# Another written-out order for an attention section of 958 steps, with three kinds of step free to change engine

## The chip, the cores and the metric

The kernel runs on one core of one Trainium2 chip. The time is the device time of one execution in microseconds (us). The engines are TensorE (PE; PEld is its weight load), VectorE (DVE), ScalarE (ACT), GpSimd (POOL) and SyncE (SP, which here only issues DMA transfers). L432 is line 432 of the kernel.

## The reference, cut to what matters

Two layers on an activation of 256 tokens by 1024 features, all in float32. Layer 0 is a gated linear recurrence and a squared-ReLU MLP. Layer 1 is sparse attention and a second MLP. A final norm follows.

```python
for i in range(DEPTH):                       # DEPTH = 2
    h = _rmsnorm(x, norm_mix[i])
    x = x + (_rglru_mixer(h, ...) if i % 2 == 0 else _nsa_mixer(h, ...))
    h = _rmsnorm(x, norm_ffn[i])
    x = x + _sq_relu_mlp(h, ...)             # relu(h @ w_up)**2 @ w_down
return _rmsnorm(x, norm_final)

# _nsa_mixer, 16 heads of 64 in 4 key/value groups
q, kv, gates = split(h @ w_in)
k_c, v_c = compress(kv[0]), compress(kv[1])  # blocks of 32 tokens, stride 16: gelu(flat @ w1) @ w2
p_c = softmax(q @ k_c - alibi);  p_s = softmax(q @ k_selected - alibi);  p_w = softmax(q @ k_window - alibi)
o = g0 * p_c @ v_c + g1 * p_s @ v_s + g2 * p_w @ v_w
return o @ w_out
```

With 256 tokens the window (512) and the selection (16 blocks of 64) leave no token out, so both branches differ only in keys, values and gates.

## The kernel before

**Products.** Activations lie with features on the 128 partitions and the 256 tokens along the free dimension. A float32 product is made of two parts of each operand: `hi`, the value rounded to the type that the matmul takes, and `lo`, the residue. `mm3` (L432 to L434) runs three matmuls per product (hi hi, hi lo, lo hi). A piece of weights (128x1024) is read from HBM into one of five `raw` buffers by a DMA on SyncE's queue (`load`, L365), its `hi` is a cast (L445, by ScalarE or VectorE), its `lo` a subtraction on VectorE (L442).

**The section.** The whole of layer 1's attention, from the projections to the first products of the following MLP, is one `Section`. `add(engines, cost, function, r, w, t)` registers a step, with the keys that it reads and writes, from which the dependencies follow; a step may list two engines. `emit(ORDER)` then issues the 958 steps one by one as the string `ORDER` (L59 to L92) names them; a `'` behind the number takes the step's second engine. The costs and the times `t` play no part in it. Each engine runs its own steps in that order, and so does each DMA queue: a step that must wait holds up all behind it on its engine.

```python
for x in seed.split():
    who, fn = self.tasks[int(x.rstrip("'"))][:2]
    fn(self.engines[who[x[-1] == "'"][0]])
```

**The steps of attention.** The projections (q, k, v and the two inputs of the compressed branch) are `mm3` products of weight pieces. Keys (`kh`, `kl`) and queries (`sa`, `sb`, with hi and lo) are scaled, cast and subtracted into place or first into `th` and `tl`, and then brought to the other partition half by DMA moves of 64 KB, issued by SyncE (L480). For each pair of head and branch group a step of scores (L1316, L1317) fills a bank of PSUM, VectorE adds the position bias and finds the row's extreme (L1323), ScalarE takes the exponential and the row sum (L1326), the probabilities `pt` are scaled (L1345, on either engine), transposed by TensorE (L1356) into a bank, copied to `pth` (L1359, ScalarE), their residue subtracted to `ptl` (L1360, VectorE), and multiplied by the values (L1381, L1383). The compressed branch adds its product into the same bank (L1253 for its scores, L1294 and L1388 for its values).

A pair of heads leaves its two half results in one bank: the lower head's result needs the upper partitions of one column block and the lower ones of the other. So for each half a copy (L1392, ScalarE) brings one block across the partitions into the tile `osum`, and an add (L1395, VectorE) adds the other block. `osum` is then split into `oh` (L445) and `ol` (L442) and goes into the output product, whose result is added to the residual `xt` (L659).

**The norm after it.** For each of the eight feature blocks: `hh`, the block scaled by the norm's weights (L570, ScalarE), its residue (L571, VectorE), a square (L574, ScalarE; the last block on VectorE) and its sum into `acc` (L581, VectorE). The MLP's first up projections run on the unscaled activation while `stats` (L643) sums `acc` over the partitions, and the scaling factor is spread by a product (L648).

Steps that the text names: 648, 738, 653 and 696 are score products; 637 the compressed branch's scores of a later pair; 851, 878 and 880 are L1392 copies of the last two pairs, 878 and 880 the two of the last; 935 a square of the norm; 27, 28, 36, 38, 39, 48, 253 casts of 64x256 into keys or queries; 514 and 621 casts of 128x256 into `th`; 139, 402, 859, 860 rescales of 128x128 and 140, 141 of 128x256; 244, 927, 967, 983, 1009 weight casts; 282 and 283 copies of the compressed hidden values; 758, 885, 965, 973 loads of weights; 581, 624, 627, 629 moves of two query blocks.

Of the kernel before, what the change touches and what calls it, by code (L numbers as in the profile page):

```python
# [14 lines left out]
AF = mybir.ActivationFunctionType  # L15
OP = mybir.AluOpType
# [39 lines left out]
551' 553 547 526 540 557 543 552 563 544 558 548 565 555 567 556 569 559 560 561 562  # L56
"""
ORDER = """
1 4 11 19 7 10 20 2 21 3 22 30 88 12 75 13 31 14 82 15 181 89 32 16 33 17 23 90 98 91 24' 83 92 41 27 18 42 34 194 29 43  # L59
38' 223 99 28 44 25 50 45 242 26 51 46 36' 164 35' 69 47 37 52 165 53 64 54 321 59 67 93 55 62 95 48 60 70 56 183 65 72  # L60
71 39 184 74 57 77 66 118 61 79 119 376 123 121 120 49 73 126 76 40 196 81 124 78 58 68 80 197 153 225 148 84 151 426 86
156 127 149 85 226 110 87 157 207 94 114 108 97 122 480 109 244' 101 128 152 96 129 100 150 111 132 102 6 323 130 133
208 134 103 210 135 9 131 105 0 166 125 154 63 107 115 155 104 136 142 106 137 211 140' 167 139' 378 245 168 141 169 143
116 175 505 324 138 185 428 161 170 158 566 112 146' 186 145' 162 144' 113 187 159 429 174 188 173 198 189 172 176 163
199 193 379 200 482 201 160 612 190 227 117 678 178' 192 202 217 228 483 507 229 171 191' 230 205 204' 246 231 203 247
147' 234' 235 248 508 206 249 218 232 212 233' 325 568 250 213 220 255 215 251 219 209 569 253 256 614 257 252 221 615
216 258 179 177 222 268 259 326 261 269 214 260 273 262 180 263 254 327 270 236 264 276 328 265 271 277 266 237 380 267
329 680 285' 278 330' 283' 370 333 274 279 373 282 281 284 381 280 335 331 272 681 240 286 336 275 338 241 299 310 290
238 758 287 291 382 311 300 288 292 313 430 301 312 289 315 296 383 314 302 293 297 349 716 303 354 384 294 304 239 340
350 385 305 357 341 306 390 355 371 352 392 431 307 374 394 885 356 308 410 375 432 351 397 309 411 358 316 484 413 395  # L70
317 353 298 423 386 414 399 318 295 433 388 319 400 372 424 469 925 402' 718 320 485 434 425 342 401 719 359 435 472 343
440 444 412 420 360 509 445 403 361 345 344 438 486 421 362 346 404 436 415 363 422 760 487 447 364 418 455 365 347 488
366 419 416 456 367 489 348 474 417 368 492 494 457 477 475 369 470 570 490 458 405 449 478 406 495 571 450 476 460 442
451 479 407 452 534 497 461 408 572 535 459 471 409 573 454' 462 537 536 473 904 464 510 574 538 784 463 453 524 467 575
511 465 527 468 525 512 466 539 528 580 540 526 499 513 887 761 588 585 529 586 616 500 514 532 501 530 541 515 503 519
531 587 542 520 617 589 888 522 543 631 533 618 517 544 632 965 619 590 545 502 633 581 596 504 620 591 927 583 560 634
546 576 592 549 561 621 594 599 564 622 597 563 550 593 626 648 658 562 551 629 651 595 552 685 649 635 578 553 565' 547
# [6 lines left out]
840 823 800 792 839 831' 807 793 822 824 789 794 796' 803 825 801 842 797' 832 795 828' 808 804 843 829' 830 845 844 790  # L84
731 802 846 835 863 841 833 848 847 805 732 834 866 791 836 849 806 864 857 850 858 865 867 917 862 861' 859' 909 860
868 853 809 869 851 872 854 870 889 852 873 871 896 947 874 875 967' 975 948 876 855' 856 877 983' 910 880 890 878 881
918 879 929 882' 930 883 897 968 919 891 931 892 911 1007 932 898 893 912 937 895 899 991 984 938 939 900 958 933 901
# [3 lines left out]
"""  # L91
ROUNDS, SHIFT, MOVES, SPREAD = 6, 1.5, 12, 3.0  # L92
HPEN, LPEN, APEN, LEAD = 0.56, 1.0, 0.0, 9.0
# [50 lines left out]
class Plan:  # L144
# [9 lines left out]
    def add(self, eng, dur, fn=None, r=(), w=(), t=0.0, lag=None):  # L154

        if fn is None:
            eng, fn = eng, dur
        if isinstance(eng, str):
            eng = [(eng, dur, 0.0)]
        i, deps = len(self.tasks), set()  # L160
        for k in r:
            if k in self.writer:
                deps.add(self.writer[k])
            self.readers.setdefault(k, []).append(i)
        for k in w:
            deps.update(self.readers.pop(k, ()))
            if k in self.writer:
                deps.add(self.writer[k])
            self.writer[k] = i
        deps.discard(i)  # L170
        self.tasks.append((eng, fn, sorted(deps), t, lag))
# [158 lines left out]
def trunk_kernel(ctx: ExitStack, tc: tile.TileContext, x_in, vec_in, const_in, w2_in, wts, out):  # L330
    nc = tc.nc
    ctx.enter_context(tc.manual_schedule())
    pe, dve, act, pool = nc.tensor, nc.vector, nc.scalar, nc.gpsimd
# [110 lines left out]
    def copy(o, a):  # L444
        return lambda e: (e.copy if e is act else e.tensor_copy)(o, a)  # L445
# [7 lines left out]
    class Section:  # L453
# [112 lines left out]
        def norm(self, m, gcol, t):  # L566

            g = vec[:, gcol + m:gcol + m + 1]
            xk = [("xt", m)]
            self.add("act", 0.4, lambda e: e.activation(hh[:, m], xt[:, m], AF.Identity, scale=g), r=xk, w=[("hh", m)], t=t)  # L570
            self.add("dve", 0.4, lambda e: e.scalar_tensor_tensor(  # L571
                hl[:, m], xt[:, m], g, hh[:, m].bitcast(F32), op0=OP.mult, op1=OP.subtract), r=xk, w=[("hh", m)], t=t)
            dst, dk = (acc, "acc") if m == 0 else (sqs[m % 2], ("sq", m % 2))
            sq = lambda e: (e.activation(dst, xt[:, m], AF.Square) if e is act else  # L574
                            e.tensor_tensor(dst, xt[:, m], xt[:, m], op=OP.mult))
            if m == KC - 1:
                self.add("dve", 0.34, sq, r=xk, w=[dk], t=t)
                return
            self.add("act", 0.31, sq, r=xk, w=[dk], t=t + 0.3)
            if m:  # L580
                self.add("dve", 0.34, lambda e: e.tensor_tensor(acc, acc, dst, op=OP.add), r=[dk], w=["acc"], t=t + 0.6)  # L581

# [401 lines left out]
    with ExitStack() as ph:  # L984
# [363 lines left out]
        def transposes(s, t):  # L1348
            pt = pts[s % NPT]
            for b in range(2):  # L1350
                bk = [("ps", 5 + b)]
                tp = zview(("tp", s, b), 5 + b, lambda x: x[:, :3 * P])

                def run(e, tp=tp, b=b):
                    for i, o in enumerate((b * P, 2 * P + b * S, 2 * P + b * S + P)):
                        e.transpose(tp()[:, i * P:(i + 1) * P], pt[:, o:o + P], identf)  # L1356
                add("pe", 0.25, run, r=[("pt", s % NPT, qc, b) for qc in range(2)], w=bk, t=t)
                i = s // 2 * 4 % NTH + 2 * b + s % 2
                add("act", 0.37, lambda e, tp=tp, i=i: e.copy(pth[i], tp()), r=bk, w=[("pth", i)], t=t + 0.3)  # L1359
                add("dve", 0.47, lambda e, tp=tp, i=i: e.tensor_tensor(ptl[i], tp(), pth[i].bitcast(F32),  # L1360
                                                                       op=OP.subtract),
                    r=bk + [("pth", i)], w=[("ptl", i)], t=t + 0.4)

        def pv(pr, t):
# [24 lines left out]
                             stop=i == 1)  # L1389
            add("pe", 0.24, run_c, r=[("bdh", a), ("bdl", a), ("pc", a % 2)], w=bk, t=t + 1.4)  # L1390
            for hf in range(2):
                add("act", 0.34, lambda e, hf=hf: e.copy(x[own_(hf)], o()[own_(1 - hf), hf]), r=bk,  # L1392
                    w=[("osum", pr % 2, hf)] + ([("bd", pr)] if pr < 2 else []),
                    t=t + 1.5)
                add("dve", 0.34, lambda e, hf=hf: e.tensor_tensor(x[own_(hf)], x[own_(hf)], o()[own_(hf), hf], op=OP.add),  # L1395
                    r=bk, w=[("osum", pr % 2, hf)], t=t + 1.6)
# [219 lines left out]
```

## The time and the profile before

| | before |
|---|---|
| median of 3 runs | 558.59 us (558.42 to 559.39) |
| the profiled execution | 559.15 us, span 557.4 us |
| granted TensorE clock, mean | 0.996 |
| PE busy | 546.1 us (98%), 3878 instructions |
| DVE busy | 455.6 us (82%), 950 instructions |
| ACT busy | 385.9 us (69%), 794 instructions |
| the section on the span's axis | 257.6 to 390.5 us |

The profile is that of one execution, whose time (559.15 us) is the span (557.4 us) and 1.75 us around it. Busy time is that of an engine's instructions laid over each other, so a pipelined engine can read as busy while it waits a little. In a row of the timeline stand the start in us, the duration in us, the engine, the line, the operation, what it writes and reads, the shape and the count; in square brackets the time that the engine stood idle before, and what ended it (inferred). In a row grouped by shape the busy time and the mean duration in ns of one stand behind the bar, and behind the next bar the idle time before them. A window's row has the length, the busy time and count of each engine, the granted clock, the busy share of the DMA engines and what they moved. A row of DMA issues ends with the median time from issue to landing.

### The profile page before, as it was taken

To read this page: it belongs to the slowest core of one execution; us is meant where nothing else is said; L and a number is where in the kernel's file an instruction comes from. 1 tells how busy PE (TensorE), PEld (TensorE's weight loads), DVE (VectorE), ACT (ScalarE), POOL (GpSimd) and SP (SyncE) were. 2 spreads that over 40 slices of the span, in tenths; PEclk is the share of its full clock that TensorE was granted. 3 is DMA by queue.
4 is the path that set the end of the run, shared out by engine and by line. 5 is a ranking of instruction groups with operands and counts; after the bars stand their busy time and mean duration, and the time that the engine had idled before them with its cause. 6 is when DMAs were issued, how large, how long until landed. Compare 5 with 4: busy or idle time off the path is not lost.

```text
span 557.4 us, 10574 instructions
## 1 busy us (share of the span) xinstructions
PE 546.1 (98%) x3878; PEld 515.4 (92%) x3878; DVE 455.6 (82%) x950; ACT 385.9 (69%) x794; POOL 51.4 (9%) x67
## 2 busy tenths in 40 slices
PE   9999999999999999999999998999999999999994
PEld 8999999999999999999999997999999999999994
DVE  6999999999995674776999999999999996564532
ACT  7899756788775543545899999977788775453420
POOL 1220000000000211311000101000000000132220
PEclk9999999999999999999999999999999999999998
DMA  8976454876565466566750857424776666467402
GB/s 302 367 213 227 152 198 164 254 234 232 196 210 200 161 216 220 165 198 200 265 179 16 222 152 238 96 42 156 250 235 234 212 196 229 151 197 210 160 1 75
DMA packets 32899, 106.24 MB, mean 191 GB/s; under 512 B 4016, under 2 KB 6976, under 8 KB 32848
## 3 DMA queue, kind: packets, MB, share of 16 engines
q1 hardware_dynamic: 30496, 98.65, 53.4%
q0 software_dynamic: 1776, 6.39, 5.0%
q8 instruction: 30, 0.49, 0.3%
q10 hardware_dynamic: 576, 0.53, 0.3%
q14 instruction: 21, 0.17, 0.1%
HBM read 102.41 MB, written 1.05 MB: 186 GB/s over the span
## 4 chain that ended last, share of the span: by engine, by line
PE 86%; DVE 6%; ACT 4%; DMA 3%; issue 1%; SPq 0%; DVEq 0%; ACTq 0%
PE bank L438 35%; PE bank L439 18%; PE bank L432 9%; PE bank L434 9%; PE bank L433 9%; ACT pt L1326 1%; PE bank L832 1%; DMA raw<-in_dram 1%; DVE whl L442 1%; PE bank L1356 1%; DVE pt L1323 1%; DMA xt<-in_dram 1%; PE bank L1188 1%; PE bank L1186 1%; ACT pth L1359 1%
## 5 line engine op out<-in xcount | busy, mean ns | idle before, releaser
L388 DVE TENSOR_TENSOR whl<-raw,whl 128x1024 fp32r<-128x1024 f32 x117 | 146.4, 1271 | 5.1 <-ACT whl L379 3.1
L438 PE MATMUL bank<-hhl,whl 128*128 128x512 f32 x456 | 149.5, 382 | 0.0
L438 PE MATMUL bank<-uhl,whl 128*128 128x512 f32 x448 | 146.8, 382 | 0.0
L379 ACT CAST whl<-raw 128x1024 fp32r<-128x1024 f32 (+1 forms) x118 | 120.5, 1046 | 7.8 <-ACT whl L379 5.6
L439 PE MATMUL bank<-hhl,whl 128*128 128x256 f32 x456 | 124.3, 273 | 0.0
L439 PE MATMUL bank<-uhl,whl 128*128 128x256 f32 x448 | 122.1, 273 | 0.0
L438 PEld LDWEIGHTS bank<-hhl,whl 128*128 128x128 f32 x456 | 86.2, 189 | 12.0
L438 PEld LDWEIGHTS bank<-uhl,whl 128*128 128x128 f32 x448 | 84.7, 189 | 11.7
L432 PE MATMUL bank<-hhl,whl 128*128 128x256 f32 x312 | 87.6, 281 | 0.0
L439 PEld LDWEIGHTS bank<-hhl,whl 128*128 128x128 f32 x456 | 87.6, 192 | 0.0
L434 PE MATMUL bank<-hhl,whl 128*128 128x256 f32 x312 | 86.0, 276 | 0.2 <-DVE whl L442 0.2
L439 PEld LDWEIGHTS bank<-uhl,whl 128*128 128x128 f32 x448 | 86.0, 192 | 0.0
L433 PE MATMUL bank<-hhl,whl 128*128 128x256 f32 x312 | 86.0, 276 | 0.0
L442 DVE TENSOR_TENSOR whl<-raw,whl 128x1024 fp32r<-128x1024 f32 (+3 forms) x69 | 72.7, 1072 | 0.5 <-ACT whl L445 0.3
L659 DVE TENSOR_TENSOR xt<-xt,bank 128x256 f32<-128x256 f32 x39 | 15.7, 417 | 62.4 <-ACT part L966 58.8
L433 PEld LDWEIGHTS bank<-hhl,whl 128*128 128x128 f32 x312 | 59.7, 191 | 0.5 <-DVE hhl L710 0.2
L434 PEld LDWEIGHTS bank<-hhl,whl 128*128 128x128 f32 x312 | 59.7, 191 | 0.4 <-DVE whl L442 0.4
L432 PEld LDWEIGHTS bank<-hhl,whl 128*128 128x128 f32 x312 | 59.8, 192 | 0.2
L445 ACT CAST whl<-raw 128x1024 fp32r<-128x1024 f32 (+2 forms) x55 | 52.0, 956 | 7.0 <-PE bank L433 3.6
L966 ACT COPY part<-bank 128x256 f32<-128x256 f32 x14 | 5.2, 373 | 61.8 <-PE bank L439 61.8
L938 ACT ACTIVATE u<-t 128x256 f32<-128x256 f32 x64 | 26.7, 418 | 15.4 <-DVE t L936 9.9
L931 ACT COPY b<-bank 128x256 f32<-128x256 f32 x57 | 20.7, 362 | 13.8 <-PE bank L439 13.7
(233 smaller groups left out, 1020.4 us busy)
## 6 DMA issues: line engine op xcount, KB each, us to landing
raw<-in_dram SPq DMA_DIRECT2D x171, 512.0 KB, 4.3
whl<-in_dram POOLq DMA_DIRECT2D x8, 512.0 KB, 5.5
raw<-in_dram SPq DMA_DIRECT2D x5, 256.0 KB, 5.2
xt<-in_dram SPq DMA_DIRECT2D x4, 256.0 KB, 4.5
gw<-in_dram POOLq DMA_DIRECT2D x2, 512.0 KB, 6.5
gw<-in_dram SPq DMA_DIRECT2D x2, 512.0 KB, 6.6
gl<-in_dram POOLq DMA_DIRECT2D x2, 512.0 KB, 7.5
zwol<-in_dram SPq DMA_DIRECT2D x2, 512.0 KB, 6.7
```

The source lines that it names most:

```text
L379: (act.copy if eng is None else eng.tensor_copy)(hi_t[i % NSPL][:, :n], raw_t[i % NRAW][:, :n])
L388: (eng or dve).tensor_tensor(lo[:, :n], raw_t[i % NRAW][:, :n], hi[:, :n].bitcast(F32), op=OP.subtract)
L432: pe.matmul(ps, wh, xh, start=start, stop=False)
L433: pe.matmul(ps, wh, xl, start=False, stop=False)
L434: pe.matmul(ps, wl, xh, start=False, stop=stop)
L438: pe.matmul(z.rearrange("p (i b a) -> p i b a", i=2, a=2), wh, xd, start=start, stop=False)
L439: pe.matmul(pairs(z[:, :S]), wl, xd[:, 0], start=False, stop=stop)
L442: return lambda e: e.tensor_tensor(o, a, h.bitcast(F32), op=OP.subtract)
L445: return lambda e: (e.copy if e is act else e.tensor_copy)(o, a)
L659: dve.tensor_tensor(two(xt[:, m]), two(xt[:, m]), nat(z), op=OP.add)
L931: act.copy(two(b), nat(z[:, S:]))
L938: act.activation(u, t, AF.Square)
```

## The change

Only the section of attention is touched. Four kinds of step that ran on ScalarE alone may now run on VectorE as well: the scaling of the norm, its square, the copy of the transposed probabilities, and the copy of the value sums. And the string `ORDER` is another arrangement of the same 958 numbers, 23 of which take another engine than before:

- from ScalarE to VectorE: 27, 28, 39, 48, 253, 514, 141, 860, 282, 1009, and, by the new freedom, 851, 878 and 935;
- from VectorE to ScalarE: 36, 38, 139, 140, 402, 859, 283, 244, 967, 983.

No step 570 (`hh`) and no copy of probabilities takes VectorE in the new string.

```diff
@@ ORDER
-1 4 11 19 7 10 20 2 21 3 22 30 88 12 75 13 31 14 82 15 181 89 32 16 33 17 23 90 98 91 24' 83 92 41 27 18 42 34 194 29 43
...
+4 6 19 1 11 10 7 20 2 21 22 30 88 12 75 13 31 14 15 181 89 32 16 33 17 82 23 91 34 90 41 98 39' 28' 83 42 43 35' 194 24'
...
-            self.add("act", 0.4, lambda e: e.activation(hh[:, m], xt[:, m], AF.Identity, scale=g), r=xk, w=[("hh", m)], t=t)
+            self.add([("act", 0.4, 0.0), ("dve", 0.26, 0.5)], lambda e: (
+                e.activation(hh[:, m], xt[:, m], AF.Identity, scale=g) if e is act else
+                e.tensor_scalar(hh[:, m], xt[:, m], g, None, op0=OP.mult)), r=xk, w=[("hh", m)], t=t)
...
-            self.add("act", 0.31, sq, r=xk, w=[dk], t=t + 0.3)
+            self.add([("act", 0.31, 0.0), ("dve", 0.34, 0.5)], sq, r=xk, w=[dk], t=t + 0.3)
...
-                add("act", 0.37, lambda e, tp=tp, i=i: e.copy(pth[i], tp()), r=bk, w=[("pth", i)], t=t + 0.3)
+                add([("act", 0.37, 0.0), ("dve", 0.47, 0.5)], lambda e, tp=tp, i=i: copy(pth[i], tp())(e), r=bk, w=[("pth", i)],
+                    t=t + 0.3)
...
-                add("act", 0.34, lambda e, hf=hf: e.copy(x[own_(hf)], o()[own_(1 - hf), hf]), r=bk,
+                add([("act", 0.34, 0.0), ("dve", 0.34, 0.5)], lambda e, hf=hf: copy(x[own_(hf)], o()[own_(1 - hf), hf])(e), r=bk,
```

Where the new string places what the text speaks of, old first:

```
loads among SyncE's moves   333 331 336 338 758 390 392 885 397 ...      ->  758 885 331 333 336 338 925 397 392 ...
                            581 583 576 622 629 578 624 627 973 981      ->  578 583 622 576 973 629 624 581 627 981
casts on ScalarE near 335   502 504 927 621 564                          ->  503 504 543 564 562 621 632 ... 600 927
products near 341           688 659 660 738 637                          ->  701 658 682 685 688 659 691 660 738 637
the last pair's halves      copies of both halves on ScalarE             ->  880 on ScalarE, then 878 on VectorE
```

More of the change, by code (lines that the diff above doesn't have):

```diff
@@ L58 @@
 ORDER = """
-1 4 11 19 7 10 20 2 21 3 22 30 88 12 75 13 31 14 82 15 181 89 32 16 33 17 23 90 98 91 24' 83 92 41 27 18 42 34 194 29 43
[L60 to L77, printed above, removed]
[6 rows of a table removed]
-840 823 800 792 839 831' 807 793 822 824 789 794 796' 803 825 801 842 797' 832 795 828' 808 804 843 829' 830 845 844 790
@@ L85 @@
-731 802 846 835 863 841 833 848 847 805 732 834 866 791 836 849 806 864 857 850 858 865 867 917 862 861' 859' 909 860
-868 853 809 869 851 872 854 870 889 852 873 871 896 947 874 875 967' 975 948 876 855' 856 877 983' 910 880 890 878 881
-918 879 929 882' 930 883 897 968 919 891 931 892 911 1007 932 898 893 912 937 895 899 991 984 938 939 900 958 933 901
[3 rows of a table removed]
+4 6 19 1 11 10 7 20 2 21 22 30 88 12 75 13 31 14 15 181 89 32 16 33 17 82 23 91 34 90 41 98 39' 28' 83 42 43 35' 194 24'
+44 37 223 26 50 164 45 27' 51 99 25 69 46 71 36 29 38 242 52 47 18 165 53 59 73 60 321 93 54 64 62 57 40 70 55 72 183 56
@@ new lines @@
+76 67 74 65 63 78 48' 66 184 77 196 118 123 119 79 376 49 61 81 126 68 80 121 197 127 84 120 85 225 148 58 86 426 124 87
+108 92 125 109 95 226 110 97 128 153 244 101 129 149 480 133 94 156 3 150 135 96 130 9 0 122 131 103 114 105 107 157 136
+111 100 323 151 102 142 137 104 154 166 143 152 115 139 144' 167 141' 138 147' 140 245 106 116 168 112 155 158 324 505
+161 378 169 185 162 566 170 159 113 212 174 117 186 215 428 163 187 175 160 188 173 146' 429 171 198 482 199 189 200 213
+192 145' 379 201 190 227 172 202 612 217 507 204' 228 678 176 191' 207 203 229 483 205 230 206 246 231 193 247 234' 235
@@ new lines @@
+210 220 208 248 233' 232 249 508 218 568 255 250 758 614 219 256 569 251 257 209 180 252 258 179 178' 615 221 268 259
+273 261 260 177 325 222 885 216 262 326 214 263 269 264 271 327 265 274 211 253' 328 270 266 254 272 267 370 276 680 373
+329 278 282' 380 236 330' 279 285' 283 331 237 284 280 381 281 239 335 333 275 681 286 277 336 238 299 338 310 240 290
[5 rows of a table added]
+407 459 534 461 408 572 497 535 454' 409 451 490 573 462 536 473 440 464 463 904 537 471 574 965 510 465 538 467 511 466
+761 468 512 453 499 575 539 524 529 887 500 527 540 513 530 528 585 514' 502 541 532 517 531 519 542 586 525 515 588 888
@@ new lines @@
+533 616 520 526 617 522 589 587 545 618 578 560 580 501 590 503 583 619 504 561 546 543 631 565' 596 564 620 549 562 544
[6 rows of a table added]
+781 764 773 737 838 765 782 752 774 779 826 789 753 770 776 780 772 766 775 754' 827 783 798 756 840 777 820 767 757 832
+792 755' 799 821 828' 793 833 839 823 796' 800 822 794 807 824 797' 795 831' 842 825 801 808 803 802 843 845 804 790 830
+844 846 835 805 829' 863 847 836 848 834 806 849 732 841 791 864 866 857 858 850 865 867 909 859 861' 860' 862 917 868
+853 851' 869 872 854 870 889 852 873 871 896 947 874 875 809 855' 948 876 856 877 918 880 878' 897 967 879 910 881 929
@@ L91 @@
+983 882' 930 883 890 968 898 891 911 892 931 1007 912 919 893 932 937 913 920 894 938 921 899 939 975 984 958 959 900
[3 rows of a table added]
 """
```

23 rows, old and new, of the table ORDER are left out of this document.

## The prediction

> **What bounds the kernel now.** I read the page's first part and its chain shares, then five windows over the attention section, then the rows by tile shape, then the timelines of TensorE, VectorE and SyncE where TensorE stops.
>
> ```profile
> PE 546.1 (98%) x3878; PEld 515.4 (92%) x3878; DVE 455.6 (82%) x950; ACT 385.9 (69%) x794; POOL 51.4 (9%) x67
> PE 86%; DVE 6%; ACT 4%; DMA 3%; issue 1%; SPq 0%; DVEq 0%; ACTq 0%
> ```
>
> TensorE is busy 98% of the span and carries 86% of the chain that ended last. The edit touches only the 958 steps between 257.6 and 390.5 us, so the whole page says little; the section's own windows say more.
>
> ```profile
> core 0: us, PE busy (x) PEld busy (x) DVE busy (x) ACT busy (x) POOL busy (x), PEclk, DMA share, GB/s
> 257.60:295.70 38.10, 37.94 (x322) 37.33 (x322) 36.40 (x94) 33.41 (x73) 1.00 (x7) 1.00 0.62 208
> 295.70:315.20 19.50, 19.33 (x162) 18.73 (x161) 19.05 (x77) 18.18 (x59) 0.57 (x1) 1.00 0.39 107
> 315.20:344.20 29.00, 27.69 (x217) 25.60 (x215) 27.93 (x109) 28.15 (x88) 1.98 (x3) 1.00 0.70 194
> 344.20:370.70 26.50, 25.95 (x201) 24.46 (x202) 25.60 (x107) 25.97 (x83) 3.09 (x4) 1.00 0.35 89
> 370.70:390.50 19.80, 19.75 (x177) 19.55 (x176) 18.63 (x38) 12.19 (x24) 0.09 (x1) 1.00 0.52 144
> sum 132.90, PE 130.65 PEld 125.67 DVE 127.61 ACT 117.91 POOL 6.72; mean PE 26.13 PEld 25.13 DVE 25.52 ACT 23.58 POOL 1.34
> ```
>
> Three engines are full at once. From 315.2 to 344.2 us TensorE is busy 27.69 of 29.00, VectorE 27.93, ScalarE 28.15; in the next window all three lack about 0.5 to 0.9. TensorE's visible idle time is 132.90 - 130.65 = 2.25 us for the section, 1.31 and 0.55 of it in these two windows. Its work does not change with the order, so 2.25 is roughly what an order can win; the busy time of a pipelined matmul can hide some waiting, so it is not a hard ceiling. The clock is 1.00 throughout, so nothing is to be had from it.
>
> The stops are at score products (L1316), which need a bank emptied by the VectorE reduction at L1323. The last column is the engine's own idle time:
>
> ```profile
> 336.11 0.35 PE L1316 MATMUL bank<-kh,sb 128*128 128x256 f32 x1 [0.40 <-PE bank L1253]
> 340.50 0.46 PE L1316 MATMUL bank<-kh,sa 128*128 128x512 f32 x1 [0.58 <-PE bank L1388]
> 344.24 0.48 PE L1316 MATMUL bank<-kh,sb 128*128 128x512 f32 x1 [0.30 <-DVE pc L1297]
> 346.14 0.45 PE L1316 MATMUL bank<-kh,sb 128*128 128x512 f32 x1 [0.51 <-DVE mx L1323]
> ```
>
> Together 0.40 + 0.58 + 0.30 + 0.51 = 1.79 us. Two of them name TensorE itself as releaser, long done; by the code it is the reduction that empties the bank.
>
> **The change part by part.** The order strings hold the same 958 steps with the same dependencies. *Moved between engines.* Of the new freedoms only three are used: two bank copies of the value sums (steps 851 and 878, L1392) and one square of the norm (935, L574). No copy of probabilities and no scaling step leaves ScalarE. Twenty steps that already had a choice change engine too. Prices by shape:
>
> ```profile
> L445 ACT CAST whl<-raw 128x1024 fp32r<-128x1024 f32 x47 | 48.7, 1044 | 6.7 <-PE bank L433 3.6 <-DMA raw<-in_dram 2.2 <-ACT whl L379 0.8
> L445 DVE CAST whl<-raw 128x1024 fp32r<-128x1024 f32 x8 | 5.5, 687 | 0.0
> L445 ACT CAST kh<-tt 64x256 fp32r<-64x256 f32 x4 | 1.6, 404 | 0.1
> L445 DVE CAST kh<-tt 64x256 fp32r<-64x256 f32 x4 | 1.1, 287 | 0.1
> L445 ACT CAST th<-tt 128x256 fp32r<-128x256 f32 x6 | 2.4, 398 | 0.0
> L1345 ACT ACTIVATE pt<-pt,sm 128x256 f32<-128x256 f32 x21 | 10.3, 502 | 0.0
> L1345 ACT ACTIVATE pt<-pt,sm 128x128 f32<-128x128 f32 x20 | 7.7, 395 | 0.1
> L1345 DVE TENSOR_SCALAR pt<-pt,sm 128x256 f32<-128x256 f32 x11 | 3.8, 348 | 0.1
> L1345 DVE TENSOR_SCALAR pt<-pt,sm 128x128 f32<-128x128 f32 x12 | 3.2, 277 | 0.0
> L1392 ACT COPY osum<-bank 64x256 f32<-64x256 f32 x16 | 5.9, 367 | 0.9 <-PE bank L1388 0.6
> L1395 DVE TENSOR_TENSOR osum<-osum,bank 64x256 f32<-64x256 f32 x16 | 6.7, 418 | 1.6 <-ACT osum L1392 1.2
> L574 ACT ACTIVATE sq<-xt 128x256 f32<-128x256 f32 x12 | 4.8, 410 | 3.5 <-DVE acc L581 3.3
> ```
>
> To VectorE go five 64x256 casts (27, 28, 39, 48, 253; 5 x 0.287 = 1.44), one 128x256 cast (514; between the 64x256 cast and the rescale, 0.29 to 0.35), a 128x256 and a 128x128 rescale (0.348 + 0.277), the two value copies (no VectorE row; between the cast's 0.287 and the add's 0.418, so 0.57 to 0.84), the square (taken as the add, 0.42) and one weight cast (1009; 0.687): 4.03 to 4.36 us. From it go two 64x256 casts (0.57), three 128x128 and one 128x256 rescale (0.83 + 0.35) and three weight casts (244, 967, 983; 2.06): 3.81. VectorE gains 0.2 to 0.55 us of work. ScalarE loses 5 x 0.404 + 0.398 + 0.502 + 0.395 + 2 x 0.367 + 0.410 + 1.044 = 5.50 and takes 2 x 0.404 + 3 x 0.395 + 0.502 + 3 x 1.044 = 5.63. (Steps 282 and 283, equal copies, change places.) This is an exchange, not relief of either full engine.
>
> *The start.* VectorE's queue waits twice for others at 264 and 270 us:
>
> ```profile
> 264.08 0.48 DVE L1035 SCALAR_TENSOR_TENSOR tt<-bank,cst,rstd 128x256 f32<-128x256 f32 x1 [0.25 <-PE bank L434]
> 269.89 1.23 DVE L442 TENSOR_TENSOR whl<-raw,whl 128x1024 fp32r<-128x1024 f32 x1 [0.29 <-ACT whl L445]
> ```
>
> The casts 28 and 39 now stand ahead of these steps and fill the 0.54 us, so VectorE runs up to 0.5 ahead from 270 on. TensorE can use little of it there: its idle time to 295.7 is 38.10 - 37.94 = 0.16. I take -0.15; bounds 0 and -0.32, twice the idle time, for waits that pipelined matmuls hide.
>
> *The score waits.* The casts and rescales that changed engine ahead of 336 us cancel on VectorE: 5 x 0.287 + 0.3 + 0.348 = 2.08 come, and 2 x 0.287 + 2 x 0.277 + 0.348 + 0.687 = 2.16 go. What is left is what the order itself moves past the four reductions: one step of value residue and two small reductions go behind the first (-0.5 net, a rescale comes ahead), a reciprocal of the softmax sums stands ahead of the second (+0.1), a compressed-branch reduction ahead of the third (+0.2), and the two that free the fourth change places (0 to +0.66, taken as +0.3). With the 0.5 of lead they come free 1.0, 0.4, 0.3 and 0.2 earlier. Waits on one engine share what is won: what the first gives back is used up when the next waits for the same engine. So the gain lies between that of the last, 0.2, and all the waits, 1.79. I take -0.5, near the low end, because the work ahead of the last three grows.
>
> *The value sums.* Both copies of a pair write one tile, and the adds behind them wait for both:
>
> ```profile
> 371.12 0.74 ACT L1392 COPY osum<-bank 64x256 f32<-64x256 f32 x2 [0.56 <-PE bank L1388]
> 371.90 0.85 DVE L1395 TENSOR_TENSOR osum<-osum,bank 64x256 f32<-64x256 f32 x2 [0.43 <-ACT osum L1392]
> ```
>
> Step 878 on VectorE now takes the place of one of the two ScalarE copies, with 880 ahead of it in the order. If the tile's dependency ignores partitions, 878 waits for 880 and the pair takes as long as before: 0.36 + 0.3 to 0.4. Casts 967 and 983 leave VectorE just ahead, but its wait there shows it was early. I take 0; bounds -0.37 (one copy) and +0.1. [...]
>
> *The tail.* Behind the last lo difference VectorE takes 1009 and 935, 0.687 + 0.42 = 1.1 us. Its window has 19.80 - 18.63 = 1.17 idle, 0.43 of it the wait above, so 0.7 covers 1.1: up to 0.4 late. ScalarE, with 19.80 - 12.19 = 7.6 idle, runs 1.45 less, and the squares and scalings on it come sooner. One more projection step stands ahead of the statistics and hides some 0.67. I take -0.1; bounds -0.3 and +0.4.
>
> *DMA issues.* Weight loads 758 and 885 move ahead of four 64 KB moves near 304 us; both buffers were free by 300, so they leave earlier and nothing waits. Load 973 now stands ahead of moves 629, 624, 581 and 627:
>
> ```profile
> 332.70 0.58 SPq L365 DMA_DIRECT2D raw<-in_dram  x1
> 333.38 0.46 SPq L480 DMA_DIRECT2D sa<-tl  x1
> 338.39 0.59 SPq L480 DMA_DIRECT2D sa<-tl  x1
> 339.03 2.02 SPq L365 DMA_DIRECT2D raw<-in_dram  x4
> ...
> raw<-in_dram SPq DMA_DIRECT2D x1, 512.0 KB, 4.3
> sa<-tl SPq DMA_DIRECT2D x1, 64.0 KB, 3.8
> sa<-tl SPq DMA_DIRECT2D x1, 64.0 KB, 2.0
> 341.01 0.29 PE L1253 MATMUL bank<-kc,sa 128*128 128x32 f32 x2
> ```
>
> A move issued 0.68 us behind a load took 3.8 us (landing 337.2, just behind the load's 337.0); one behind other moves took 2.0. The moves of 973's group need casts of about 335, so the load leaves near 336.2 and lands near 340.5, and the four moves right behind it, to about 341.4. Step 738 needs 581 and the compressed product 637 needs all four, at 340.5 and 341.0 before; one output step (0.67) now stands ahead of them. So they just arrive: 0, bounds 0 and +1.0.
>
> Sum: -0.15 - 0.5 + 0 - 0.1 + 0 = -0.75 on the profiled 559.15 us (a span of 557.4 and 1.75 around it), 558.4. That execution stands 0.56 above the median of 558.59, so 557.8 against the median.
>
> **The rivals.** *Most waits go.* The order is another throughout, and the three-engine interplay may settle where I cannot see. For it: 2.25 us of idle time, 1.79 at four products. Against it: the exchange leaves both feeders as full as they were, 27.93 and 28.15 of 29. Worth about -2.0: 556.6.
> *Late moves (slower).* If the load 973 leaves later than about 336.6 (its own queue waits for moves that wait for casts), each 0.1 beyond it delays product 637 by 0.1 and TensorE stands, with the reductions and exponentials behind. At 1.7 us late, net of the -0.75, it gives 559.6; at 2.2, 560.1. For it: the 3.8 us landing. Against it: the weight cast 927 (1.04 us) stood ahead of cast 621 on ScalarE and is now behind it. [...]
> *VectorE as the pace (no gain).* If the section follows VectorE's total, +0.2 to +0.55, and the tail's +0.4, the time rises 0.6 to 0.95: about 559.3.
> *The halves run side by side.* Then -0.37 more: 557.4.
>
> **How the numbers follow.** A measurement here tells 0.2% (1.1 us) from no change: faster is under 557.47, slower over 559.71. Chances: the forecast 0.45 (its own range 557.2 to 558.6), most waits go 0.26, late moves 0.14, VectorE as the pace 0.10, halves side by side 0.05. Faster: 0.26 and 0.05 and a fifth of the forecast's, 0.40. Slower: most of the late moves and some of VectorE, 0.19. Same 0.41. The range, 556.0 to 559.9, takes in the largest sum of waits less a little and the late moves at 2.0 us.
>
> **What would show it.** In the changed profile the waits at the four score products should sum to 1.2 to 1.5 us instead of 1.79; visible TensorE idle in the section to 1.5 to 1.9; VectorE's busy time to rise by under 0.6; the last value add to start no earlier against its last product than 371.90 - 371.12 = 0.78; the statistics to stand no later behind the last lo difference; and product 637 to name no move as releaser. A sum of section idle under 0.8, or a TensorE wait that ends with a 64 KB move, makes the prediction wrong.

## The result: slower by 0.75%

The changed kernel takes 563.60 us in the median (560.49 to 565.43, 6 executions) against 558.75 (558.42 to 559.39, 6): ratio 1.0075, 95% interval 1.0060 to 1.0089. The forecast was 557.8, the range 556.0 to 559.9. The executions lie in three groups, 560.5, 562.2 to 562.4, and 564.8 to 565.4, where those of before keep within 1 us. The profiled one is the fastest, 560.49 us (span 558.7), 1.34 above the profiled one of before, while the median is 4.85 above: most of the loss is in executions without a profile. (Two executions of later runs, of 2015 and 3239 us, are left out below.)

The first part of the changed kernel's page, and its windows over the section, columns as before:

```profile
PE 545.7 (98%) x3878; PEld 514.6 (92%) x3878; DVE 455.6 (82%) x953; ACT 384.7 (69%) x791; POOL 50.8 (9%) x67
```

```profile
257.60:295.70 38.10, 37.71 (x319) 36.95 (x320) 36.15 (x96) 33.06 (x71) 0.71 (x5) 1.00 0.60 208
295.70:315.20 19.50, 19.07 (x160) 18.34 (x159) 19.09 (x74) 17.88 (x61) 0.90 (x3) 1.00 0.46 136
315.20:344.20 29.00, 26.75 (x213) 25.18 (x212) 27.75 (x110) 27.67 (x86) 1.99 (x3) 1.00 0.67 184
344.20:370.70 26.50, 25.60 (x198) 23.94 (x199) 25.08 (x107) 25.35 (x81) 2.34 (x3) 1.00 0.32 79
370.70:390.50 19.80, 19.72 (x171) 19.39 (x171) 18.77 (x40) 12.23 (x23) 0.86 (x1) 1.00 0.45 132
```

Visible TensorE idle time is 0.39, 0.43, 2.25, 0.90 and 0.08: 4.05 us, against 2.25 before. TensorE's timeline in the changed kernel, the rows with idle time of 0.18 us or more to 348 us:

```profile
268.30 0.37 PE L1188 MATMUL bank<-whl,hhl 128*128 128x304 f32 x1 [0.18 <-DVE tt L1037]
279.25 0.35 PE L432 MATMUL bank<-hhl,whl 128*128 128x256 f32 x1 [0.20 <-DVE vhl L1207]
303.18 0.41 PE L1145 MATMUL bank<-hid,w2raw 128*128 128x64 f32 x2 [0.43 <-PE bank L1358]
325.11 0.38 PE L1318 MATMUL bank<-kh,sb 128*128 128x256 f32 x1 [0.18 <-DVE pc L1299]
336.10 0.35 PE L1318 MATMUL bank<-kh,sb 128*128 128x256 f32 x1 [0.56 <-PE bank L1358]
342.08 0.45 PE L1318 MATMUL bank<-kh,sa 128*128 128x512 f32 x1 [1.44 <-DVE cm L1275]
344.65 0.35 PE L1318 MATMUL bank<-kh,sb 128*128 128x256 f32 x1 [0.52 <-DVE mx L1325]
347.11 0.45 PE L1318 MATMUL bank<-kh,sb 128*128 128x512 f32 x1 [0.23 <-DVE mx L1325]
```

(L1316 of before is L1318 here.) The 0.56 us stand at step 648, the 1.44 at 738, the 0.52 at 810 (the score product between 738 and 653), the 0.23 at 696; 653, at 345.21, does not wait. SyncE's timeline and the landings, same kernel:

```profile
336.67 0.58 SPq L365 DMA_DIRECT2D raw<-in_dram  x1
337.36 0.46 SPq L480 DMA_DIRECT2D sb<-tl  x1
337.86 0.59 SPq L480 DMA_DIRECT2D sb<-th  x1
338.50 1.25 SPq L480 DMA_DIRECT2D sa<-tl  x2
...
sb<-tl SPq DMA_DIRECT2D x1, 64.0 KB, 3.8
...
sa<-tl SPq DMA_DIRECT2D x1, 64.0 KB, 3.3
```

Load 973 leaves at 336.67. Move 581, the third behind it, is issued at 338.50 and lands 3.3 us later, at 341.8; 738 starts at 342.08. By the dependencies 738 needs 581 and the bank, and not the reciprocal on VectorE that is named as releaser.

### The profile page after: what moved, and what is told of

Same layout as the page of the kernel before. It is cut to its first block, busy times and chain, and to the rows that moved or that the text cites. A ratio compares the mean times of both kernels' runs of the same rounds, so it can differ in the third digit from the quotient of the medians.

```text
span 558.7 us, 10573 instructions
## 1 busy us (share of the span) xinstructions
PE 545.7 (98%) x3878; PEld 514.6 (92%) x3878; DVE 455.6 (82%) x953; ACT 384.7 (69%) x791; POOL 50.8 (9%) x67
## 4 chain that ended last, share of the span: by engine, by line
PE 90%; DVE 5%; ACT 2%; issue 1%; DMA 1%; SPq 0%; DVEq 0%; ACTq 0%
PE bank L438 35%; PE bank L439 18%; PE bank L433 10%; PE bank L432 10%; PE bank L434 10%; PE bank L1358 1%; PE bank L834 1%; DVE whl L442 1%; PE bank L1386 1%; DMA xt<-in_dram 1%; DVE pt L1325 1%; PE bank L1318 1%; PE bank L1124 1%; PE bank L1319 1%; DVE osum L1398 1%
## 5 line engine op out<-in xcount | busy, mean ns | idle before, releaser
L445 ACT CAST whl<-raw 128x1024 fp32r<-128x1024 f32 (+2 forms) x57 | 54.0, 961 | 8.1 <-PE bank L433 5.6
L1328 ACT ACTIVATE pt<-pt,mx 128x128 f32<-128x128 f32 (+1 forms) x64 | 28.8, 453 | 1.3 <-DVE mx L1325 1.0
```

The source lines that it names most:

```text
L1328: add("act", (0.39, 0.49)[qc], lambda e, row=row, j=j: e.activation(row, row, AF.Exp, bias=mx[:, j:j + 1], scale=-1.0, accum_out=sm[:, j:j ...
```

## The experiments

The kernel before was measured again beside each group of experiments: median 558.92 us beside e1 to e4, 559.02 beside e5 to e8, 559.15 beside e9 to e12, 559.01 beside e13 to e16, 559.08 beside e17 and e18. Every ratio is to the one beside it. All lengths of a dip in the clock are read from windows of 1 us.

**One late load (e1, e2).** Edits, as neighbours on SyncE:

```diff
 # e1, changed kernel
-973 629 624 581 627
+629 624 581 627 973
 # e2, kernel before
-581 583 576 622 629 578 624 627 973
+583 576 622 973 629 578 624 581 627
```

> The changed kernel with one step moved: the weight load 973 stands behind the four 64 KB moves 629, 624, 581 and 627 again. Late-load theory: the moves land 2.0 us after issue, the wait of 1.44 us at the score product near 342 falls to about 0.5, and the time is 559.2 to 559.6 us with a granted clock of 0.996 in every execution. Exchange theory (VectorE and ScalarE loaded otherwise) and order-at-large theory: the time stays at 562 to 564 us and the clock at 0.991 to 0.993.

> The kernel before with its load 973 put ahead of the moves 629, 578, 624, 581 and 627, and move 581 behind 624, nothing else. Late-load theory: the score product near 340.5 waits 1 to 2 us for its move, the time rises by 1 to 2 us in executions with clock 0.996, and by more in those where the clock falls to 0.993 or below: 560 to 564 us. The other theories: 558.4 to 559.4 us, as before.

e2: 562.24 us (559.57 to 564.44, 12; ratio 1.0052, 1.0035 to 1.0068). e1: 562.77 (561.13 to 565.44, 6; ratio 1.0064, 1.0041 to 1.0088). So the late load alone costs the old order 3.3 us, as its theory had it, but its repair is not enough in the new one: e1 lies in the range of the other theories, 562 to 564, and its interval is not clear of the changed kernel's. TensorE in e2, then in e1:

```profile
342.46 0.45 PE L1316 MATMUL bank<-kh,sa 128*128 128x512 f32 x1 [2.31 <-DMA sa<-tl]
```

```profile
329.40 0.35 PE L1318 MATMUL bank<-kh,sa 128*128 128x256 f32 x1 [1.68 <-issue]
342.29 0.46 PE L1318 MATMUL bank<-kh,sa 128*128 128x512 f32 x1 [0.67 <-PE bank L1391]
```

In e1 the wait near 342 has fallen from 1.44 to 0.67, and one of 1.68 stands at step 524, near 329, which the changed kernel's profiled execution did not have. 524 needs move 490 (`sa<-th`). GpSimd's and SyncE's timelines and the landing in e1:

```profile
324.90 0.53 POOL L508 DMA_DIRECT2D whl<-in_dram  x1 [5.32 <-DVE pc L1299]
325.06 0.60 SPq L480 DMA_DIRECT2D sa<-th  x1
sa<-th SPq DMA_DIRECT2D x1, 64.0 KB, 4.3
```

Issued behind a 512 KB transfer of GpSimd's queue, it lands 4.3 us later, at 329.36. In the changed kernel's profiled execution 490 went at 324.47, 0.65 us ahead of that transfer (325.12), and took 2.8. Being first by a little is not enough: in e3 490 went at 326.04, 0.58 us ahead of it (326.62), and took 5.5.

e1 and e2 also show the clock. Windows of 1 us in e1:

```profile
345.00:346.00 1.00, 0.44 (x3) 0.40 (x2) 0.97 (x5) 0.98 (x4) 0.00 (x0) 0.61 1.04 418
346.00:347.00 1.00, 1.00 (x6) 1.00 (x6) 0.97 (x4) 1.00 (x3) 0.00 (x0) 0.50 1.00 401
347.00:348.00 1.00, 1.00 (x4) 0.82 (x3) 0.32 (x3) 1.00 (x3) 0.00 (x0) 0.50 0.41 152
348.00:349.00 1.00, 1.00 (x5) 0.77 (x5) 1.00 (x6) 0.93 (x4) 0.73 (x2) 0.68 0.04 16
```

The third number from the end is the granted clock: half speed for 3.4 us, 0.39 + 0.50 + 0.50 + 0.32 = 1.71 us of full-speed time lost. e2 loses 1.71 as well, from 343.9 us on.

**The other transfer (e5, e7).** Edit: 490 moved from behind 497 to ahead of 495; e5 has the edit of e1 too.

> The changed kernel with two steps moved on SyncE's queue: load 973 behind the four moves, and move 490 (a query's high part, needed by score product 524 near 328) ahead of its three neighbours, where it is issued 1 to 2 us sooner and ahead of the 512 KB casting transfer that GpSimd issues near 325. Theory of the two late moves: no wait over 0.7 us at the score products near 328 and 342, clock 0.996 in every execution, 558.8 to 559.6 us. Order-at-large theory: still 561 us or more, with waits elsewhere.

> The changed kernel with move 490 alone placed early; load 973 stays ahead of the four moves. Theory of the two late moves: the wait near 328 is gone in every execution, that of 1.4 us near 342 stays, and the time is that of the changed kernel's fastest execution, 560 to 561 us, with a clock of 0.996 in most. If the wait near 342 alone brings the clock down, 562 us or more.

e7: 562.51 (560.42 to 562.97, 6; ratio 1.0051, 1.0038 to 1.0064): no execution is near 565, in line with 490 as the cause of those; the 1.4 us near 342 stays, its profile has a dip, and the time is the one forecast for the case that this wait alone brings the clock down. e5: 562.63 (561.09 to 563.54, 5; ratio 1.0066, 1.0053 to 1.0079), span 559.3 in its profile. No wait over 0.67 is left, which was foreseen, but the clock falls in that execution all the same (1.70 us from 345.2), and the time is over the 561 of the order-at-large theory. TensorE in e5 ahead of it:

```profile
341.02 0.45 PE L1318 MATMUL bank<-kh,sa 128*128 128x512 f32 x1 [0.67 <-PE bank L1391]
343.06 0.41 PE L1296 MATMUL bank<-cst,cq 128*64 128x128 f32 x2 [0.58 <-DVE cq L1278]
344.36 0.35 PE L1318 MATMUL bank<-kh,sb 128*128 128x256 f32 x1 [0.56 <-DVE mx L1325]
```

**Cover near 341 (e9, e10).** Edit: e9 is e5 with output products 701 ahead of 738 and 682 behind 637; e10 is the kernel before with 701 ahead of 658 and 682 ahead of 685, as the change has them.

> The changed kernel with both late moves mended and two output products put back as cover: 701 ahead of score product 738, 682 behind the compressed product 637. Clock theory (TensorE's waits close together from 341 to 345 us, 0.67, 0.58 and 0.56, bring the granted clock down to half for 3.4 us, a loss of 1.70 us): the three waits fall below 1.0 together, the clock stays 0.995 or more in most executions, and the time is 559.0 to 560.0 us. Rival (the clock falls for another reason, or the waits only move): 561.5 us or more, a mean clock of 0.991 to 0.994.

> The kernel before with only these two output products moved early, as the change has them: 701 ahead of 658 and 682 ahead of 685. Clock theory: the waits from 340 to 346 grow by 0.3 to 0.6 together, the clock falls in a part of the executions, and the median is 559.5 to 561.5 us. Rival: 558.6 to 559.4 us, the clock as before.

e9: 561.12 (560.16 to 562.33, 8; ratio 1.0038, 1.0027 to 1.0049), 1.5 us under e5, no dip in its profile, but between its two forecasts. e10: 560.02 (559.35 to 561.56, 11; ratio 1.0016, 1.0007 to 1.0025), 0.9 slower than before; its wait at 738 is 0.99 instead of 0.58, and no dip in the profile. So the early place of the two products is a part of the loss in these two orders (in e18, below, putting them back gained nothing).

**Engines (e3, e4, e6, e8).** Four kinds of step were set free, not three as the title says, and two of them are used. e3: the changed order, all 23 steps on their old engines. e4 and e6: the old order, all 23 on the new ones (the rows below are of e6). e8: the old order with 851, 878 and 935 alone.

> The changed kernel's order with every step on the engine that it had before (23 steps go back). Late-load theory: no better than the changed kernel, 562 to 565 us. Exchange theory: faster than it by 1 us or more, 558.8 to 561 us.

> The order of before with the 23 steps on the engines of the changed kernel, so also a pair of value-sum copies split over ScalarE and VectorE. Late-load theory: 558.3 to 559.3 us. Exchange theory: 560 us or more.

> The order of before with all 23 steps on the new engines, once more for a profile, since the profile taken first is of an execution four times as long. Expected: a span near 562 us at clock 0.996 (five executions gave 563.3 to 564.0 us), and a wait of some us at one place before 345 us, where a cast that changed engine stands behind others in its new queue.

> The order of before with only the three new freedoms used: the value-sum copies 851 and 878 and the square 935 on VectorE. If VectorE's copy in the tail or at the last pair is what costs the order of before with all new engines its 5 us: 561 us or more. If it is one of the twenty older exchanges: 558.4 to 559.4 us.

e3: 565.51 (564.25 to 566.10, 6; ratio 1.0106, 1.0089 to 1.0122), the slowest of all. e4: 563.3 to 564.0 in five executions (ratio 1.0076, 1.0062 to 1.0091); e6: 564.39 in its single execution. e8: 559.24 (558.63 to 560.90, 11; ratio 1.0005, 0.9997 to 1.0014), no change. TensorE in e6:

```profile
274.64 0.45 PE L1318 MATMUL bank<-kh,sb 128*128 128x512 f32 x1 [0.82 <-DVE mx L1325]
376.84 0.38 PE L432 MATMUL bank<-oh,whl 128*128 128x256 f32 x1 [1.17 <-DVE oh L445]
```

The exchange theory is half met. e4 came out as it had it (560 us or more); e3, which it expected 1 us or more faster than the changed kernel, is 1.9 slower. So the exchange costs the old order some 4.7 us and the new order nothing, and the three new freedoms alone cost nothing in the old one. The wait that e6 was to show ahead of 345 us is not there (none over 0.62 from 300 to 345). In e6 the casts 967 and 983 have joined another ahead of the last pair's copy on ScalarE, and I take the 1.17 us to follow from that; ScalarE in e6:

```profile
371.77 2.94 ACT L445 CAST whl<-raw 128x1024 fp32r<-128x1024 f32 x3
374.74 0.36 ACT L445 COPY osum<-bank 64x256 f32<-64x256 f32 x1
```

The two waits of e6 are 1.99 of the 4.2 us by which its span is longer; the rest is not traced. The old order with the new engines misses the late-load theory's 558.3 to 559.3 by over 4 us, so "late transfers alone" was too narrow as well.

**Where in the section (e11, e12, e14, e15).** Each takes one order (with its engines) up to a step and the other for all that is left: e11 the new up to 299 (306 us), then the old; e12 the old up to 299, then that of e9; e14 the old up to 549 (335 us), then that of e9; e15 that of e9 up to 549, then the old.

> The changed kernel's order up to step 299 (near 306 us) with its engines, then the remaining steps as the kernel before has them. The changed kernel is 0.6 us later at the hidden product near 303. If the head costs just that: 559.3 to 560.0 us with a clock of 0.996. If what the head leaves behind shifts the later waits so that the clock falls: 561 us or more.

> The old order up to step 299 with the old engines, then the changed order with both late moves mended and the two output products put back. If the head's 0.6 us and the clock's 1.70 us are all that is left of the loss: 558.4 to 559.2 us, level with the kernel before or faster. If the rest of the new order is worse by itself: 560 us or more.

> The steps up to 549 (near 335 us) in the order and on the engines of the kernel before, the rest as in the mended new order (load 973 behind the four moves, 701 and 682 as cover). If what is left lies between 306 and 335: 558.6 to 559.6 us. If it lies in the new order behind 335: 560.5 us or more.

> The converse: up to 549 the mended new order (move 490 early), the rest as in the kernel before. The head costs 0.4 us. If what is left lies between 306 and 335: 560.5 to 561.5 us. If it lies behind 335: 559.3 to 560 us.

| cut | median (range, n) | ratio, 95% |
|---|---|---|
| e11: new to 306, old behind | 559.58 (559.25 to 560.27, 11) | 1.0007, 0.9998 to 1.0015 |
| e14: old to 335, new behind | 559.96 (559.50 to 561.25, 11) | 1.0016, 1.0007 to 1.0025 |
| e15: new to 335, old behind | 561.55 (559.97 to 562.27, 6) | 1.0032, 1.0019 to 1.0044 |
| e12: old to 306, new behind | 562.13 (561.23 to 565.20, 6) | 1.0061, 1.0043 to 1.0080 |

The head costs 0.4 us, which is not clear of noise; what is behind 335, about 0.9 (e14 lies between its two forecasts); and the stretch from 306 to 335 most, 561.55 - 559.58 = 2.0. e12 came out as its second alternative had it: with the old head the rest is no better than in e9. These are costs of pieces in their surroundings and do not add exactly.

**What happens from 306 to 335 (e13, e17, e18).** e13 is e9 with move 440 ahead of 490 and the cast 514 back on ScalarE. e17 is the changed kernel with SyncE's 62 transfers in the sequence of before and all other engines unchanged; e18 the same with 701 and 682 put back.

> The kernel with both late moves mended and the two output products put back (the run before: 561.1 us, clock 0.996), and now also move 440 placed ahead of 490 and the cast 514 back on ScalarE. On VectorE 514 stood 0.4 to 0.8 us until 440, which reads the buffer that 514 overwrites, had landed. If that third late move is what is left in the middle: VectorE's wait near 330 is gone and the time is 0.4 to 0.8 us lower, 560.2 to 560.8 us. If not: 561 us or more.

> The changed kernel with all 62 transfers on SyncE's queue in the sequence of the kernel before; every other engine keeps the changed sequence and the changed choice of engine. Theory that the transfers' sequence is the loss: no wait of a score product near 328 or 342 for a move, no wait of VectorE or ScalarE for a staging buffer near 330, and 559.4 to 560.5 us (0.4 us stay for the head), without executions over 562. If the sequence on the compute engines is the loss: 561.5 us or more.

> The same, with output products 701 and 682 also put back as cover near 341. If the waits of the changed order near 341 to 345 are a loss of their own that these two cover: 0.3 to 0.8 us under the run without them, level with the kernel before plus the head's 0.4, 559.0 to 559.8 us. If they only move the waits: equal to it within 0.3 us.

e13: 562.71 (560.50 to 564.25, 6; ratio 1.0060, 1.0042 to 1.0077), 1.6 us over e9, though the intervals just overlap. e17: 563.29 (562.54 to 563.95, 6; ratio 1.0071, 1.0056 to 1.0085). e18: 563.04 (561.31 to 564.42, 6; ratio 1.0068, 1.0050 to 1.0086), equal to e17 within the 0.3 us that stood for waits that only move. The theory that the sequence of SyncE's transfers is the loss falls. e17, with the old sequence, has the late landings all the same; GpSimd, SyncE's issue and landing of 490, ScalarE and TensorE:

```profile
321.01 0.56 POOL L508 DMA_DIRECT2D whl<-in_dram  x1 [2.44 <-PE bank L434]
326.89 0.53 POOL L508 DMA_DIRECT2D whl<-in_dram  x1 [5.33 <-DVE pc L1299]
...
325.60 0.59 SPq L480 DMA_DIRECT2D sa<-th  x1
...
sa<-th SPq DMA_DIRECT2D x1, 64.0 KB, 4.9
...
330.55 0.40 ACT L445 CAST th<-tt 128x256 fp32r<-128x256 f32 x1 [0.90 <-DMA sa<-th]
330.84 0.35 PE L1318 MATMUL bank<-kh,sa 128*128 128x256 f32 x1 [1.14 <-DMA sa<-th]
```

Here 490 goes ahead of the later of the two transfers of GpSimd, behind the earlier one, and still takes 4.9 us.

I read it so: the moves are late because the steps that make the data of the moves ahead of them are late. Those are a cast into `th` on ScalarE and a residue into `tl` on VectorE, of keys; in the kernel before:

```profile
315.47 0.40 ACT L445 CAST th<-tt 128x256 fp32r<-128x256 f32 x1
315.90 0.42 DVE L442 TENSOR_TENSOR tl<-tt,th 128x256 fp32r<-128x256 f32 x1
```

and the same two steps (435 and 444) in the changed kernel:

```profile
317.71 0.41 ACT L445 CAST th<-tt 128x256 fp32r<-128x256 f32 x1
320.31 0.42 DVE L442 TENSOR_TENSOR tl<-tt,th 128x256 fp32r<-128x256 f32 x1
```

They come 2.2 and 4.4 us later. The six moves that carry them, and the query moves among and behind them, fill SyncE's queue until 326.2 instead of 324.2, a transfer of GpSimd goes near 325.2 in both, and the moves that come last meet it. Mending one move made another the last: 490 in e1, 440 for the cast 514 in e9, 492 in e13, for which a cast on ScalarE stood 1.80 us.

That the two steps' place is the cause is an inference from these rows; putting them back alone was not tried. And GpSimd's own sequence had changed too: its load 784 stood behind load 904 and now stands ahead of it. GpSimd in the kernel before, then in the changed kernel:

```profile
325.22 1.08 POOL L508 DMA_DIRECT2D whl<-in_dram  x2 [8.73 <-PE bank L434]
```

```profile
319.24 0.56 POOL L508 DMA_DIRECT2D whl<-in_dram  x1 [2.44 <-PE bank L434]
325.12 0.54 POOL L508 DMA_DIRECT2D whl<-in_dram  x1 [5.33 <-DVE pc L1299]
```

Of two transfers that went together behind SyncE's moves, one now goes 6 us earlier, among the moves. e17 leaves this as the change has it, so it is a rival to the two steps' place that no run tells apart.

**A wait by itself (e16).** The kernel before with step 928 doubled on VectorE.

> The kernel before with one subtraction on VectorE, the lo of a weight piece (step 928, 1.22 us near 339), done twice, so that the score product near 340.5 waits 1.2 us longer. Clock theory (waits of some 1.8 us within four us bring the granted clock to half for 3.4 us): 1.2 us plus, in most executions, 1.7 us: 561 to 562.5 us, with a dip of the clock in the profile a few us behind the wait. Rival (only the wait counts): 559.5 to 560.4 us, no dip.

560.28 (559.51 to 563.64, 11; ratio 1.0024, 1.0010 to 1.0037), 1.3 us above before. TensorE waits as meant:

```profile
341.09 0.45 PE L1316 MATMUL bank<-kh,sa 128*128 128x512 f32 x1 [1.84 <-issue]
```

No dip in this execution, and two of the others are over 561 (561.92 and 563.64). So the rival is met: a wait of 1.84 us did not bring the clock down in the profiled execution nor, to judge by the times, in most of the others. The median rises by about what the wait grew, 1.84 - 0.58 = 1.26 us.

## Why the prediction was wrong

*What failed.* The step that failed is the one on DMA issues, "they just arrive: 0, bounds 0 and +1.0". It followed one load and took the issue times of all other transfers from the old profile. I compared SyncE's sequence, and not the steps that make the data: 435 and 444 come 2.2 and 4.4 us later, and moves that were not themselves put behind a load land late (490 took 4.3 us in e1, 5.5 in e3 and 4.9 in e17, against 2.0 in the kernel before). Late moves held up step 524 by 1.68 us in the profiled execution of e1, 2.32 in e3 and 2.22 in e18; the sum has no term for that, and none for the 1.7 us that a fall of the clock costs. One wait and one fall are 3.4 us, and e1's profiled execution, which has both, took 562.69. The changed kernel's groups at 562.3 and 565 would fit that, but no profile of one of those executions exists, so this is argued. What delays the moves, the two steps or GpSimd's load, stays open.

*DMA issues, the part that was worked out.* The load was to leave near 336.2 and left at 336.67; move 581 landed at 341.8, where all four were to land by 341.4; 738 waited 1.44 us instead of the old 0.58, 0.86 more, inside the bounds. With the load put back (e1) 0.67 is left, so some 0.77 is the load's. This is in kind the rival that I gave 0.14, but not in size: by its rule a load 0.07 behind the threshold of 336.6 costs 0.07 us. (At 1.7 and 2.2 us late its times are 559.5 and 560.0, not 559.6 and 560.1.) The move right behind the 512 KB load (`sb<-tl`, issued at 337.36) took 3.8 us again. Nor did a second queue keep the moves quick: in e1 490 and 440, issued at 325.06 and 325.70 behind GpSimd's transfer of 324.90, took 4.3 and 4.0 us, where 490 had taken 2.0 in the kernel before.

*Score waits (-0.5).* The four products 648, 738, 653 and 696 were to wait 1.2 to 1.5 us instead of 1.79 and wait 0.56 + 1.44 + 0 + 0.23 = 2.23. Without 738, where most of the growth is the load's, the other three fell from 1.21 to 0.79, near the forecast. But a fifth, 810, which did not wait before, now waits 0.52, by the profile for a reduction on VectorE, and takes this back. 810 in the kernel before, then 653 in the changed one:

```profile
343.23 0.28 PE L1316 MATMUL bank<-kh,sb 128*128 128x256 f32 x1
```

```profile
345.21 0.48 PE L1318 MATMUL bank<-kh,sb 128*128 128x512 f32 x1
```

Of the signs that I had named, two failed: the section's visible idle time is 4.05 us and not 1.5 to 1.9, and a TensorE wait ends with a 64 KB move.

*The start (-0.15).* Not found. The head's 0.4 us in e11 are not clear of noise, but the rows point the other way: the hidden product near 303 waits 0.43 instead of 0.17, and two projections wait 0.18 and 0.20 that did not.

*The value sums (0).* Right, within the bounds. Copy 878 on VectorE waited for 880 on ScalarE:

```profile
372.36 0.37 ACT L445 COPY osum<-bank 64x256 f32<-64x256 f32 x1 [1.50 <-PE bank L1391]
...
372.76 0.43 DVE L445 COPY osum<-bank 64x256 f32<-64x256 f32 x1 [0.72 <-ACT osum L445]
373.22 0.85 DVE L1398 TENSOR_TENSOR osum<-osum,bank 64x256 f32<-64x256 f32 x2
374.11 0.29 DVE L445 CAST oh<-osum 128x256 fp32r<-128x256 f32 x1
```

From the first copy to `oh` it is 374.11 - 372.36 = 1.75 us; before, 372.79 - 371.12 = 1.67. The rival that both halves run side by side did not come about, and no run shows the 0.37 us of its term: VectorE's copy starts at 372.76, when ScalarE's (372.36 and 0.37 long) has ended, and in the profiles of e1, e5, e9 and e12 it waits 0.72 us for ScalarE's as well.

*The exchange and the tail (0.2 to 0.55 of work, -0.1).* The page gives 455.6 us of busy time on VectorE for both kernels, in 953 instructions instead of 950. Kernels with the same work on VectorE differ by as much in their profiles (455.3 in e2, which has the old engines), so the added work cannot be read from it. e8 shows the copies and the square at no cost. From the last pair's first copy to the product that spreads the scaling factor it takes 19.44 us instead of 19.33: the tail is about 0.1 slower, not 0.1 faster. Neither is the loss.

*The clock.* I wrote that it is 1.00 throughout the section and that nothing is to be had from it, and put it at nothing. Something was to be lost, 1.7 us a time in eight profiles.

## What to carry to other kernels

When an order is rearranged, follow each transfer back to the step that makes its data and forward to the step that may overwrite the buffer; a queue whose own sequence is unchanged can still be late (in e17 move 490 took 4.9 us). Compare the sequence of every queue, not of one. Keep small moves that a product waits for ahead of large loads, on their own queue and on the others, with some us of room: behind a load on their own queue one took 3.8 us here, behind GpSimd's transfer 4.3, and 0.58 us ahead of it 5.5, against 2.0; and the steps that fed them drifted by 2.2 and 4.4. In a section where three engines are full, an order and its choice of engines are one thing: the old order with the new engines was as slow as the whole change (563.3 to 564.0 against 563.60), the new order with the old engines slower than both whole ones (565.51).

## What the hardware showed that I had not expected

TensorE's clock fell to half (0.50 in windows of 1 us) inside the section in the profiled execution of eight experiments (e1, e2, e3, e5, e7, e13, e15, e17), and in neither profile of before and of the changed kernel. (In those two it falls at the end of the span, at 552.9 and 554.6 us, 1.8 and 2.2 us behind TensorE's last product; their means of 0.996 come of that.) Each time in the section it lasted about 3.4 us and cost 1.70 or 1.71 us of full-speed time. Just ahead of it stood one wait of 1.4 to 2.3 us (e2, e3, e7, e13, e15), or two or three of 0.56 to 0.67 within 3.5 us (e1, e5, e17). But like waits passed without it (1.44 and 0.52 in the changed kernel, 1.84 in e16, 2.22 in e18), so a wait does not decide. Nor does the mean clock of an execution show a fall in the section, since it counts the end too: four of e10's read 0.991 and took 559.35 to 560.24 us.

The longest single wait just ahead of a fall was the 2.31 us of e2, and in e7 1.38 stood there. How much idle time is enough, and where it has to lie, no run shows.
